# The last FFN's second product by Strassen's seven half products, with the sums on GpSimd

## The chip, the core and the metric

The program runs on one core of one Trainium2 chip. A core has TensorE for matmuls (PE in the profile, its weight loads PEld), VectorE (DVE), ScalarE (ACT), GpSimd (POOL) and SyncE (SP, which here only issues transfers). The engines run beside each other, each takes its own instructions in the order of its queue, and semaphores make one wait for another. Operands lie in SBUF, sums of matmuls in the eight banks of PSUM (128 rows of 512 float32 each), and weights come by DMA from the chip's memory. The metric is the device time of one execution, in microseconds.

## What is computed

A two-layer trunk over 512 tokens of width 1024: a gated short convolution, a dense FFN, a Mamba-2 mixer, a dense FFN. Norms, a scale, a shift and a gate stand around each. Only the second FFN (i = 1) is touched. Everything is float32.

```
D_FF = 2816

def swiglu_ffn(h, w_in, w_out):
    gate, up = jnp.split(h @ w_in, 2, axis=-1)
    return (jax.nn.silu(gate) * up) @ w_out

h = rmsnorm(x, norm_g[i, 2]) * (1.0 + scale) + shift
y = swiglu_ffn(h, f_w_in[i], f_w_out[i])
x = x + gate * rmsnorm(y, norm_g[i, 3])
```

## The kernel before

Every large product is made with float32r operands and keeps float32's accuracy by a split: a value v is cast to hi (float32r) by ScalarE, and VectorE subtracts, lo = v - hi. A product is then three matmuls into the same PSUM bank: hi by hi, hi by lo, lo by hi (lines 259 to 261 in `mm3`, 359 to 361 in `mm_tiles`). `split_w` (lines 202 and 203) splits a piece of 1024 columns of weights.

The last FFN is `ffn(3, 1, ...)`. Its first product goes over 22 blocks of 128 hidden values, two at a time (a pair): `load_w` fetches gate and up columns, `in_chunk` makes 8 x 3 matmuls of 512 tokens for each block of each half, 24 matmuls a chunk and four chunks a pair. `ff_act` applies silu on ScalarE (line 826), multiplies by up on VectorE (827), and splits the hidden value into hi and lo (829, 830). All 22 split blocks stay in SBUF.

The second product, 512 tokens x 2816 by 2816 x 1024, is `out_begin` and `out_finish`. It runs in two halves of 512 output columns. In each half four PSUM banks hold the four token tiles of 128, and the loop goes over the 22 blocks: `load_wo` fetches up to four blocks of 128 x 512 weights (1 MB, issued by SP), splits them two blocks at a time, and each block makes 4 x 3 matmuls: stationary a 128 x 128 piece of the hidden block, moving 512 columns of weights. That is 22 x 4 x 2 x 3 = 528 matmuls. The last two blocks of the first half and the last four of the second are ordered token tile by token tile (`finish`), so that the square sums (`sq`), the gate product (`yg_`), the root (`b1`, `rt1`, `rc1`), the update of x (`x`) and its store of one tile stand beside the matmuls of the next.

The order on TensorE is that of the code where `manual_schedule` names it, elsewhere the tile framework's scheduler sets it; it also sets the order on ScalarE, VectorE, GpSimd and SP around the second product. Buffers come from pools that rotate: `wst` (two), `whl` (four), `h0` to `h7` (the split input of the first product), `t2` (four). GpSimd has nothing to do after the constants at the start.

Of the kernel before, what the change touches and what calls it, by code (L numbers as in the profile page):

```python
# [35 lines left out]
def trunk_kernel(  # L36
# [75 lines left out]
    xt = [hp.tile([P, D], F32, name=f"x{t}", tag=f"x{t}") for t in range(4)]  # L112
# [172 lines left out]
    def small(n):  # L285
        return tmp.tile([P, n], F32, tag=f"ss{n}", name="ss", bufs=8)
# [257 lines left out]
    with ExitStack() as ph:  # L544
# [18 lines left out]
        h = [hp.tile([P, 2, T], F32R, tag=f"h{j}", name=f"h{j}") for j in range(4)]  # L563
        rows = actp.tile([P, 8, P], F32, tag="a", name="rows")
# [254 lines left out]
        def ffn(s, i, begun, act_tile, gg_tile, xn_tile, ada, gates, lead, after):  # L819
            w1, w2 = f_w_in[i], f_w_out[i]  # L820
            acts = []
            h, lead_ps, rest, more = begun

            def ff_act(psg, psu, f):
                g = t2("g")
                act.activation(g, psg, AF.Silu)  # L826
                dve.tensor_mul(g, psu, g)  # L827
                a = act_tile(f"ff{f}")
                act.copy(a[:, 0, :], g)
                dve.tensor_tensor(a[:, 1, :], g, a[:, 0, :].bitcast(F32), SUB)  # L830
# [34 lines left out]
    with ExitStack() as ph:  # L865
# [359 lines left out]
        with tc.manual_schedule(engines={PE_ENGINE}):  # L1225
# [56 lines left out]
```

## Time and profile before

| | us |
|---|---|
| median of 3 runs (lowest, highest) | 1391.58 (1391.44, 1391.78) |
| span of the profiled execution | 1390.8 |
| PE busy in it | 1368.9 (98%) |
| PEld busy | 1148.8 (83%) |
| DVE busy | 832.2 (60%) |
| ACT busy | 552.4 (40%) |
| POOL busy | 1.5 (0%) |

The span runs from the first to the last instruction of one profiled execution; the profile gives no other time of that execution, and the median of the runs is 0.8 us above it. PE's busy time counts matmuls that overlap, so it says whether TensorE has work, not how fast it goes; for that, starts are compared. The mean granted clock over the span is 0.996 of full. A share of the whole span mixes many stages; the stage in question is the last 125 us. In rows of the views, "L203" is a line of the kernel, out<-in are tile names, x is a count, "us, ns" are the sum and the mean of one instruction, and behind the second bar stands how long the engine was idle before them and what ended that.

### The profile page before, as it was taken

To read this page: it belongs to the slowest core of one execution; us is meant where nothing else is said; L and a number is where in the kernel's file an instruction comes from. 1 tells how busy PE (TensorE), PEld (TensorE's weight loads), DVE (VectorE), ACT (ScalarE), POOL (GpSimd) and SP (SyncE) were. 2 spreads that over 40 slices of the span, in tenths; PEclk is the share of its full clock that TensorE was granted. 3 is DMA by queue.
4 is the path that set the end of the run, shared out by engine and by line. 5 is a ranking of instruction groups with operands and counts; after the bars stand their busy time and mean duration, and the time that the engine had idled before them with its cause. 6 is when DMAs were issued, how large, how long until landed. Compare 5 with 4: busy or idle time off the path is not lost.

```text
span 1390.8 us, 17396 instructions
## 1 busy us (share of the span) xinstructions
PE 1368.9 (98%) x7039; PEld 1148.8 (83%) x7039; DVE 832.2 (60%) x1332; ACT 552.4 (40%) x827; POOL 1.5 (0%) x11
## 2 busy tenths in 40 slices
PE   8999999999999999999799999999999999999998
PEld 7788889888888888898688888888898888888886
DVE  5777756488775222759878888876673333332224
ACT  5432247222222211745765466643573222322212
POOL 0000000000000000000000000000000000000000
PEclk9999999999999999999999999999999999999999
DMA  9956671368683223415244432423413223322221
GB/s 313 317 175 223 221 239 42 120 210 287 219 272 122 91 91 98 118 48 179 70 133 136 129 98 83 131 76 107 137 60 106 91 91 101 109 93 91 91 91 61
DMA packets 154037, 190.35 MB, mean 137 GB/s; under 512 B 5845, under 2 KB 110949, under 8 KB 152933
## 3 DMA queue, kind: packets, MB, share of 16 engines
q1 hardware_dynamic: 149952, 176.47, 39.2%
q10 hardware_dynamic: 4004, 12.77, 2.8%
q8 instruction: 55, 0.90, 0.3%
q14 instruction: 26, 0.20, 0.1%
HBM read 186.98 MB, written 2.24 MB: 136 GB/s over the span
## 4 chain that ended last, share of the span: by engine, by line
PE 66%; DVE 1%; issue 0%; DVEq 0%; ACT 0%; ACTq 0%
PE ip L259 11%; PE ip L261 11%; PE ip L260 11%; PE y L359 8%; PE y L360 8%; PE y L361 8%; PE li L259 2%; PE li L261 2%; PE li L260 2%; PE yd L1092 1%; PE yo L1086 1%; PE cb L1036 1%; PE xtr L460 1%; PE ssg L1114 0%; PE xtok L1019 0%; PE st L1051 0%
## 5 line engine op out<-in xcount | busy, mean ns | idle before, releaser
L259 PE MATMUL ip<-h,whl 128*128 128x512 f32 x1096 | 434.2, 396 | 2.7 <-DVE cv L777 2.7
L261 PE MATMUL ip<-h,whl 128*128 128x512 f32 x1096 | 429.4, 392 | 6.6 <-DVE whl L203 6.6
L260 PE MATMUL ip<-h,whl 128*128 128x512 f32 x1096 | 428.2, 391 | 0.0
L261 PEld LDWEIGHTS ip<-h,whl 128*128 128x128 f32 x1096 | 206.6, 188 | 50.7 <-DVE whl L203 7.0
L259 PEld LDWEIGHTS ip<-h,whl 128*128 128x128 f32 x1096 | 206.8, 189 | 47.7 <-issue 5.6
L260 PEld LDWEIGHTS ip<-h,whl 128*128 128x128 f32 x1096 | 206.7, 189 | 43.2 <-issue 1.2
L203 DVE TENSOR_TENSOR whl<-wst,whl 128x1024 fp32r<-128x1024 f32 (+1 forms) x163 | 177.2, 1103 | 101.4 <-ACT whl L202 101.2
L202 ACT CAST whl<-wst 128x1024 fp32r<-128x1024 f32 (+1 forms) x163 | 152.1, 951 | 201.0 <-PE ip L261 121.6
L203 DVE TENSOR_TENSOR whlo<-wsto,whlo 128x1024 fp32r<-128x1024 f32 x68 | 83.3, 1225 | 181.3 <-ACT whlo L202 181.3
L202 ACT CAST whlo<-wsto 128x1024 fp32r<-128x1024 f32 x68 | 71.5, 1051 | 200.6 <-PE y L361 162.2
L359 PE MATMUL y<-whlo,ff 128*128 128x512 f32 x352 | 137.0, 389 | 0.0
L361 PE MATMUL y<-whlo,ff 128*128 128x512 f32 x352 | 136.9, 389 | 0.0
L360 PE MATMUL y<-whlo,ff 128*128 128x512 f32 x352 | 136.9, 389 | 0.0
L126 DVE SCALAR_TENSOR_TENSOR ada_acc<-ada_st,csil,ada_acc 128x512 f32<-128x512 f32 x140 | 104.8, 750 | 22.9 <-DMA ada_st<-in_ada_w_dram 20.0
L259 PE MATMUL li<-h,whl 128*128 128x256 f32 x288 | 83.2, 289 | 0.0
L827 DVE TENSOR_TENSOR g<-ip,g 128x512 f32<-128x512 f32 x40 | 27.6, 691 | 92.5 <-PE ip L261 92.4
L261 PE MATMUL li<-h,whl 128*128 128x256 f32 x288 | 81.6, 283 | 0.0
L260 PE MATMUL li<-h,whl 128*128 128x256 f32 x288 | 81.5, 283 | 0.0
L826 ACT ACTIVATE g<-ip 128x512 f32<-128x512 f32 x36 | 21.6, 599 | 145.9 <-PE ip L261 145.9
L361 PEld LDWEIGHTS y<-whlo,ff 128*128 128x128 f32 x352 | 66.1, 188 | 13.8
L359 PEld LDWEIGHTS y<-whlo,ff 128*128 128x128 f32 x352 | 66.1, 188 | 13.7
L360 PEld LDWEIGHTS y<-whlo,ff 128*128 128x128 f32 x352 | 66.1, 188 | 13.6
(215 smaller groups left out, 1623.2 us busy)
## 6 DMA issues: line engine op xcount, KB each, us to landing
ada_st<-in_ada_w_dram SPq DMA_DIRECT2D x96, 512.0 KB, 5.8
wst<-in_f_w_in_dram SPq DMA_DIRECT2D x44, 1024.0 KB, 5.2
wsto<-in_f_w_out_dram SPq DMA_DIRECT2D x20, 1024.0 KB, 4.9
wst<-in_m_w_in_dram SPq DMA_DIRECT2D x14, 1024.0 KB, 5.4
wst<-in_m_w_in_dram SPq DMA_DIRECT2D x20, 512.0 KB, 5.0
wst<-in_a_w_in_dram SPq DMA_DIRECT2D x9, 1024.0 KB, 6.2
csb<-cs_d ACTq DMA_DIRECT2D x8, 1024.0 KB, 6.2
wsto<-in_m_w_out_dram SPq DMA_DIRECT2D x7, 1024.0 KB, 4.9
```

The costliest lines, as they stand in the source:

```text
L126: dve.scalar_tensor_tensor(acc, w, csil[:, k:k + 1], acc, MUL, ADD)
L202: act.copy(dst[:, 0, :nk, :], src)
L203: dve.tensor_tensor(dst[:, 1, :nk, :], src, dst[:, 0, :nk, :].bitcast(F32), SUB)
L259: pe.matmul(dst, w_at(w, 0, kk), a[:, 0, sl], start=start, stop=False)
L260: pe.matmul(dst, w_at(w, 0, kk), a[:, 1, sl], start=False, stop=False)
L261: pe.matmul(dst, w_at(w, 1, kk), a[:, 0, sl], start=False, stop=stop)
L359: pe.matmul(pst, a[:, 0, tk], wt[:, 0, kk, :], start=k == 0, stop=False)
L360: pe.matmul(pst, a[:, 0, tk], wt[:, 1, kk, :], start=False, stop=False)
L361: pe.matmul(pst, a[:, 1, tk], wt[:, 0, kk, :], start=False, stop=k == K - 1)
L460: pe.transpose(pt[:, j * 256 + t * P:j * 256 + (t + 1) * P], self.xn[2 * hi + t][p // 2][:, c:c + P], ident)
L826: act.activation(g, psg, AF.Silu)
L827: dve.tensor_mul(g, psu, g)
```

## The change

The last FFN gets its own function, `last_ffn`. Its first product is as before, but `ff_pair` leaves the hidden values of a pair unsplit (x0 and x1, 512 tokens each), and GpSimd forms four sums of 256 columns per pair (lines 1266 to 1269 of the changed program). The second product takes the tokens in two halves of 256, the output columns in two halves of 512, and the inner dimension in 11 pairs of blocks: 2 x 2 blocks, which Strassen's algorithm (in Winograd's form) multiplies with seven half products instead of eight. A half product is two token tiles of 128 by 512 columns over 11 blocks: 2 x 3 x 11 = 66 matmuls, so 462 in all.

Six PSUM banks (pa, pb, pz, two each) cannot hold seven products, so the inner dimension is passed three times. The first pass makes three products (pa, pb, pz), and then ScalarE and VectorE copy what the other outputs need (lines 1347 to 1351). The second adds three more onto the same banks; then lines 1381 and 1382 read pb. The third adds the seventh onto pb. In the first and second pass every pair's rows of w2 are loaded (512 KB by line 1293 and 256 KB by 1294, into `raw`, three buffers), and GpSimd forms two sums of 512 columns per pair: line 1330 in place in `raw` and line 1332 from `raw` into `sums` in the first pass; 1362 in place in `raw` and 1366 from `raw` onto `sums` in the second. ScalarE and VectorE split everything for its product only then (`parts`, lines 1298 and 1299): `a6` (hidden values and their sums, in `wst`), `w8` and `w4` (weights and their sums), `a22` for the third pass. At the end the token tiles 0 and 1 are finished beside the third pass, tiles 2 and 3 behind it.

```diff
+        def ff_pair(pss):
+            xs = [pool.tile([P, T], F32, tag=f"xb{b}", name=f"xb{b}", bufs=NG2) for b in range(2)]
+            sm = pool.tile([P, 3, 256], F32, tag="sm", name="sm", bufs=NG2)
+            for b in range(2):
+                g = t2("g")
+                act.activation(g, pss[b], AF.Silu)
+                dve.tensor_mul(xs[b], pss[2 + b], g)
+            pool_tt = nc.gpsimd.tensor_tensor
+            pool_tt(sm[:, 0, :], xs[0][:, hi], xs[1][:, hi], SUB)
+            pool_tt(sm[:, 1, :], sm[:, 0, :], xs[0][:, lo], SUB)
+            pool_tt(sm[:, 2, :], sm[:, 1, :], xs[1][:, lo], ADD)
+            pool_tt(xs[0][:, hi], xs[0][:, lo], xs[0][:, hi], SUB)
...
+        def load_rows(g, b):
+            st = pool.tile([P, 3, T], F32, tag="raw", name="raw", bufs=3)
+            dma(st[:, 0:2, :], w2[rows(g, b), :].rearrange("p (a f) -> p a f", a=2))
+            dma(st[:, 2, :], w2[rows(g, 1 - b), T:])
+            return st
+        def parts(src, dst):
+            act.copy(dst[:, 0], src)
+            dve.tensor_tensor(dst[:, 1], src, dst[:, 0].bitcast(F32), SUB)
...
+        def narrow(early=False):
+            if early:
+                return whl_p.tile([P, 2, T], F32R, tag="whl", name="w4")
+            ring[0] += 1
+            return hp.tile([P, 2, T], F32R, tag=f"h{ring[0] % KD}", name="w4")
...
+        def product(acc, a, i, w, first, last):
+            for t in range(2):
+                sl = slice(t * P, (t + 1) * P)
+                pe.matmul(acc[t], a(0, i, sl), w[:, 0, :], start=first, stop=False, skip_group_check=True)
+                pe.matmul(acc[t], a(0, i, sl), w[:, 1, :], start=False, stop=False, skip_group_check=True)
+                pe.matmul(acc[t], a(1, i, sl), w[:, 0, :], start=False, stop=last, skip_group_check=True)
...
+            for g in range(NG2):
+                st = load_rows(g, 0)
+                a6 = wst_p.tile([P, 2, 3, 256], F32R, tag="wst", name="a6")
+                parts(x0s[g][:, lo], a6[:, :, 0, :])
+                parts(sums[g][:, 0:2, :], a6[:, :, 1:3, :])
+                nc.gpsimd.tensor_tensor(st[:, 1, :], st[:, 1, :], st[:, 0, :], ADD)
+                tw = sums[g][:, 0:2, :].rearrange("p a b -> p (a b)")
+                nc.gpsimd.tensor_tensor(tw, st[:, 1, :], st[:, 2, :], ADD)
+                w8 = whl_p.tile([P, 2, 2, T], F32R, tag="whl", name="w8")
+                parts(st[:, 0, :], w8[:, :, 0, :])
+                w4 = narrow(g < 2)
+                parts(tw, w4)
+                parts(st[:, 1, :], w8[:, :, 1, :])
...
+                product(pa, a, 0, w8[:, :, 0, :], g == 0, True)
+                product(pb, a, 2, w4, g == 0, True)
+                product(pz, a, 1, w8[:, :, 1, :], g == 0, True)
+            np1, nr1, c22 = ([keep(n) for _ in range(2)] for n in ("np1", "nr1", "c22"))
+            for t in range(2):
+                act.activation(np1[t], pa[t], AF.Copy, scale=-1.0)
+            for t in range(2):
+                dve.tensor_tensor(nr1[t], np1[t], pb[t], SUB)
+            for t in range(2):
+                act.copy(c22[t], pz[t])
...
+            for g in range(NG2):
+                st = load_rows(g, 1)
+                a6 = wst_p.tile([P, 2, 3, 256], F32R, tag="wst", name="a6")
+                parts(x1s[g][:, lo], a6[:, :, 0, :])
+                parts(x0s[g][:, hi], a6[:, :, 1, :])
+                parts(sums[g][:, 2, :], a6[:, :, 2, :])
+                w8 = whl_p.tile([P, 2, 2, T], F32R, tag="whl", name="w8")
+                parts(st[:, 0:2, :], w8)
+                nc.gpsimd.tensor_tensor(st[:, 2, :], st[:, 2, :], st[:, 1, :], ADD)
+                w4 = narrow()
+                parts(st[:, 2, :], w4)
+                tw = sums[g][:, 0:2, :].rearrange("p a b -> p (a b)")
+                nc.gpsimd.tensor_tensor(tw, tw, st[:, 0, :], ADD)
+                a22 = pool.tile([P, 2, 256], F32R, tag="xb0", name="a22", bufs=NG2)
+                parts(x1s[g][:, hi], a22)
...
+                todo = [(pa, 0, w8[:, :, 0, :]), (pb, 1, w4), (pz, 2, w8[:, :, 1, :])]
+                if g == NG2 - 1:
+                    todo = [todo[1], todo[0], todo[2]]
+                for acc, i, w in todo:
+                    product(acc, a, i, w, False, True)
...
+            for g in range(NG2):
+                w4 = narrow()
+                parts(sums[g][:, 0:2, :].rearrange("p a b -> p (a b)"), w4)
...
+                product(pb, lambda hl, i, sl, g=g: a22s[g][:, hl, sl], 0, w4, False, True)
...
+            for t in range(4):
+                if t >= 2:
+                    dve.tensor_tensor(np1[t - 2], pb[t - 2], np1[t - 2], SUB)
+                    ys[t] = (np1[t - 2], c22[t - 2])
...
     with ExitStack() as ph:
-        actp3 = ph.enter_context(tc.tile_pool(name="actp3", bufs=22, reuse_waits="tile"))
-        ffn(3, 1, begun, lambda n: actp3.tile([P, 2, T], F32R, tag="a", name=n),
-            lambda: actp3.tile([P, D], F32, tag="gg", name="gg", bufs=1), None, lambda f: None, (), None, None)
+        last_ffn(begun, ph.enter_context(tc.tile_pool(name="lf", bufs=1, reuse_waits="tile")))
```

What the scheduler made of it is seen in the engines' queues. GpSimd, in the first pass, from pair 2 on: the names are `raw` (the loaded rows; 10000, 10036, 10072, 10108 are pairs 2 to 5, and so on in steps of 36) and `sm` (the pair's sums; 8877, 9006, 9135, 9264 are pairs 2 to 5). Before, this queue held nothing behind the constants at the program's start.

```order
L1332 TENSOR_TENSOR sm_8877<-raw_10000 128x512
L1330 TENSOR_TENSOR raw_10108<-raw_10108 128x512
L1332 TENSOR_TENSOR sm_9006<-raw_10036 128x512
L1330 TENSOR_TENSOR raw_10144<-raw_10144 128x512
L1332 TENSOR_TENSOR sm_9135<-raw_10072 128x512
L1332 TENSOR_TENSOR sm_9264<-raw_10108 128x512
L1330 TENSOR_TENSOR raw_10180<-raw_10180 128x512
L1330 TENSOR_TENSOR raw_10216<-raw_10216 128x512
L1332 TENSOR_TENSOR sm_9393<-raw_10144 128x512
L1330 TENSOR_TENSOR raw_10252<-raw_10252 128x512
L1332 TENSOR_TENSOR sm_9522<-raw_10180 128x512
```

The first addition of pair g + 3, whose rows go into the buffer of pair g, stands behind the second addition of pair g and ahead of that of pair g + 1; pairs 4 and 5 have their second additions in a row, pairs 7 and 8 too.

ScalarE, in the second product. Before, the casts of `load_wo`'s pieces follow each other:

```order
L202 CAST whlo_10085<-wsto_10083 128x1024
L202 CAST whlo_10088<-wsto_10083 128x1024
L202 CAST whlo_10141<-wsto_10139 128x1024
L202 CAST whlo_10144<-wsto_10139 128x1024
L202 CAST whlo_10201<-wsto_10199 128x1024
```

Now, in the second pass (raw_10531, 10570 and 10609 are pairs 5, 6 and 7; a6_10495 is pair 4's):

```order
L1298 CAST w8_10541<-raw_10531 128x1024
L1298 CAST a22_10471<-xb1_9005 128x256
L1298 CAST w4_10584<-raw_10570 128x512
L1298 CAST w4_10623<-raw_10609 128x512
L1298 CAST a6_10495<-xb1_9134 128x256
L1298 CAST a6_10495<-xb0_9133 128x256
L1298 CAST a6_10495<-sm_9135 128x256
```

Many small casts have taken the place of a few large ones, and the weights' sum of pair 7 is cast ahead of the hidden values of pair 4.

VectorE, at the program's end. Before, behind the last token tile's matmuls (y03 and y13 are its two halves):

```order
L409 TENSOR_SCALAR ss_10584<-ss_10581 128x1
L404 TENSOR_TENSOR yg_10586<-y03_9914,gg_9781 128x512
L404 TENSOR_TENSOR yg_10602<-y13_10198,gg_9781 128x512
L417 RECIPROCAL ss_10604<-ss_10604 128x1
L421 SCALAR_TENSOR_TENSOR x3_101<-yg_10586,ss_10604,x3_101 128x512
L421 SCALAR_TENSOR_TENSOR x3_101<-yg_10602,ss_10604,x3_101 128x512
```

Now, behind the last product into pb (pb_9924 and pb_9925 are token tiles 2 and 3):

```order
L1398 TENSOR_TENSOR np1_10325<-pb_9925,np1_10325 128x512
L1406 TENSOR_TENSOR yg_10913<-c22_10328,gg_10774 128x512
L1406 TENSOR_TENSOR yg_10912<-np1_10324,gg_10774 128x512
L1410 RECIPROCAL ss_10921<-ss_10921 128x1
L1406 TENSOR_TENSOR yg_10932<-c22_10329,gg_10774 128x512
L1413 SCALAR_TENSOR_TENSOR x2_100<-yg_10913,ss_10921,x2_100 128x512
L1413 SCALAR_TENSOR_TENSOR x2_100<-yg_10912,ss_10921,x2_100 128x512
L1406 TENSOR_TENSOR yg_10931<-np1_10325,gg_10774 128x512
L1408 TENSOR_SCALAR ss_10939<-ss_10930 128x1
L1410 RECIPROCAL ss_10940<-ss_10940 128x1
L1413 SCALAR_TENSOR_TENSOR x3_101<-yg_10932,ss_10940,x3_101 128x512
L1413 SCALAR_TENSOR_TENSOR x3_101<-yg_10931,ss_10940,x3_101 128x512
```

Two token tiles stand behind the last matmul where one half of one stood.

More of the change, by code (lines that the diff above doesn't have):

```diff
@@ L1247, in trunk_kernel, with last_ffn, rows, keep @@
             begun = out_finish(parts)
+    def last_ffn(begun, pool):
+        w1, w2 = f_w_in[1], f_w_out[1]
+        h, lead_ps, rest, more = begun
+        lo, hi = HALVES
+        x0s, x1s, sums = [], [], []
+        def ff_pair(pss):
[10 more added lines that the diff above has]
+            pool_tt(xs[0][:, hi], xs[0][:, lo], xs[0][:, hi], SUB)
+            x0s.append(xs[0])
+            x1s.append(xs[1])
+            sums.append(sm)
+        NG2 = NF // 2
+        for f in range(0, NF, 2):
+            if f == 0:
+                with tc.manual_schedule(engines={PE_ENGINE}):
+                    for i in (0, 2, 1, 3, 4, 5):
+                        rest(i)
+                pss = lead_ps[:4]
+            elif f == 2:
+                pss = lead_ps[4:] + [in_chunk(w, h) for w in more]
+            else:
+                pss = [in_chunk(w, h) for w in load_w([(w1, f * P, 256)]) + load_w([(w1, DFF + f * P, 256)])]
+            ff_pair(pss)
+        def rows(g, b):
+            return slice((2 * g + b) * P, (2 * g + b + 1) * P)
+        def load_rows(g, b):
[6 more added lines that the diff above has]
+            dve.tensor_tensor(dst[:, 1], src, dst[:, 0].bitcast(F32), SUB)
+        ring = [0]
+        def narrow(early=False):
[3 more added lines that the diff above has]
+            return hp.tile([P, 2, T], F32R, tag=f"h{ring[0] % KD}", name="w4")
+        def keep(name):
+            return pool.tile([P, T], F32, tag="keep", name=name, bufs=6)
+        def product(acc, a, i, w, first, last):
[4 more added lines that the diff above has]
+                pe.matmul(acc[t], a(1, i, sl), w[:, 0, :], start=False, stop=last, skip_group_check=True)
+        ggt = []
+        with tc.manual_schedule(engines={PE_ENGINE}):
+            pa = [aux_ps("pa") for _ in range(2)]
+            pb = [aux_ps("pb") for _ in range(2)]
+            pz = [mm_ps("pz") for _ in range(2)]
+            for g in range(NG2):
[11 more added lines that the diff above has]
+                parts(st[:, 1, :], w8[:, :, 1, :])
+                def a(hl, i, sl):
+                    return a6[:, hl, i, sl]
+                product(pa, a, 0, w8[:, :, 0, :], g == 0, True)
[8 more added lines that the diff above has]
+                act.copy(c22[t], pz[t])
+            a22s = []
+            for g in range(NG2):
[13 more added lines that the diff above has]
+                parts(x1s[g][:, hi], a22)
+                a22s.append(a22)
+                def a(hl, i, sl):
+                    return a6[:, hl, i, sl]
+                todo = [(pa, 0, w8[:, :, 0, :]), (pb, 1, w4), (pz, 2, w8[:, :, 1, :])]
[3 more added lines that the diff above has]
+                    product(acc, a, i, w, False, True)
+            for t in range(2):
+                nr2 = t2("nr2")
+                dve.tensor_tensor(nr2, np1[t], pb[t], SUB)
+                dve.tensor_tensor(c22[t], nr2, c22[t], ADD)
+            ops = []
+            for g in range(NG2):
+                w4 = narrow()
+                parts(sums[g][:, 0:2, :].rearrange("p a b -> p (a b)"), w4)
+                ops.append(w4)
+                if g == 0:
+                    ggt.append(make_gg(3, lambda: pool.tile([P, D], F32, tag="raw", name="gg", bufs=3)))
+                product(pb, lambda hl, i, sl, g=g: a22s[g][:, hl, sl], 0, w4, False, True)
+            for t in range(2):
+                dve.tensor_tensor(nr1[t], nr1[t], pz[t], ADD)
+            ys = [(pa[0], nr1[0]), (pa[1], nr1[1]), None, None]
+            for t in range(4):
+                if t >= 2:
+                    dve.tensor_tensor(np1[t - 2], pb[t - 2], np1[t - 2], SUB)
+                    ys[t] = (np1[t - 2], c22[t - 2])
+                s2 = small(2)
+                yg = [t2("yg") for _ in range(2)]
+                order = (1, 0) if t >= 2 else (0, 1)
+                for hf in order:
+                    act.activation(t2("junk"), ys[t][hf], AF.Square, accum_out=s2[:, hf:hf + 1])
+                for hf in order:
+                    dve.tensor_mul(yg[hf], ys[t][hf], ggt[0][:, hf * T:(hf + 1) * T])
+                b1, s1 = small(1), small(1)
+                dve.tensor_scalar(b1, s2[:, order[0]:order[0] + 1], 1.0 / D, EPS, MUL, ADD)
+                act.activation(s1, s2[:, order[1]:order[1] + 1], AF.Sqrt, bias=b1, scale=1.0 / D)
+                dve.reciprocal(s1, s1)
+                for hf in order:
+                    c = slice(hf * T, (hf + 1) * T)
+                    dve.scalar_tensor_tensor(xt[t][:, c], yg[hf], s1, xt[t][:, c], MUL, ADD)
+                    dma(out[0, t * P:(t + 1) * P, c], xt[t][:, c])
```

## The prediction

> **What bounds the kernel now.** First the busy time by stretches, cut where the last FFN's second product begins and ends (columns: stretch, its length, then busy us and instructions of PE, PEld, DVE, ACT, POOL, then the granted clock, the DMA share and GB/s).
>
> ```profile
> 1243.00:1264.00 21.00, 21.00 (x94) 17.38 (x93) 7.16 (x8) 5.94 (x8) 0.00 (x0) 1.00 0.29 100
> 1264.00:1384.00 120.00, 120.00 (x530) 99.10 (x528) 33.94 (x41) 27.42 (x38) 0.00 (x0) 1.00 0.24 82
> 1384.00:1391.00 7.00, 0.07 (x1) 0.00 (x0) 2.17 (x4) 0.98 (x3) 0.00 (x0) 0.89 0.29 110
> ```
>
> TensorE works all 120 us of the second product at full clock, VectorE 34, ScalarE 27, GpSimd nothing. A matmul less is worth its interval there, as long as the others keep up. The groups by line give the count, the timeline the interval.
>
> ```profile
> L359 PE MATMUL y<-whlo,ff 128*128 128x512 f32 x176 | 68.5, 389 | 0.0
> L360 PE MATMUL y<-whlo,ff 128*128 128x512 f32 x176 | 68.5, 389 | 0.0
> L361 PE MATMUL y<-whlo,ff 128*128 128x512 f32 x176 | 68.5, 389 | 0.0
> ```
>
> ```profile
> 1264.23 0.39 PE L359 MATMUL y<-whlo,ff 128*128 128x512 f32 x1
> ...
> 1383.68 0.39 PE L361 MATMUL y<-whlo,ff 128*128 128x512 f32 x1
> ```
>
> 528 matmuls whose starts span 119.45 us: one every 119.45 / 527 = 0.2267 us (the 389 ns of one overlap).
>
> **What goes.** Seven products for eight leave 11 pairs x 7 x 6 = 462 matmuls of the same form: 66 fewer, 66 x 0.2267 = **15.0 us** off TensorE. A pair's three products in the first or second pass take 18 x 0.2267 = 4.08 us, a pass 44.9, the third pass 15.0.
>
> **What comes: the prices.** The splits (a cast by ScalarE, then a subtraction by VectorE) at their three widths, from the groups by line:
>
> ```profile
> L203 DVE TENSOR_TENSOR whlo<-wsto,whlo 128x1024 fp32r<-128x1024 f32 x19 | 23.3, 1226 | 75.7 <-ACT whlo L202 75.7
> L202 ACT CAST whlo<-wsto 128x1024 fp32r<-128x1024 f32 x19 | 20.0, 1054 | 82.2 <-PE y L361 74.5 <-PE ip L261 3.9 <-issue 3.9
> L830 DVE TENSOR_TENSOR ff<-g,ff 128x512 fp32r<-128x512 f32 x22 | 15.0, 685 | 2.5 <-ACT ff L829 2.5
> L829 ACT CAST ff<-g 128x512 fp32r<-128x512 f32 x22 | 13.5, 616 | 0.0
> L478 DVE TENSOR_TENSOR h<-u,h 128x256 fp32r<-128x256 f32 x3 | 1.3, 425 | 0.5 <-ACT h L474 0.5
> L474 ACT CAST h<-u 128x256 fp32r<-128x256 f32 x2 | 0.8, 407 | 1.3 <-DVE u L469 1.3
> ```
>
> A first-pass pair splits 256 + 4 x 512 columns: ScalarE 0.41 + 4 x 0.62 = 2.9 us, VectorE 0.43 + 4 x 0.69 = 3.2. A second-pass pair splits 3 x 256, 1024, 512 and 256: ScalarE 3.3, VectorE 3.6; from pair 4 on a third-pass split of 512 stands among them (3.9 and 4.3). Against 4.08 that is nearly full but hidden, and rows that follow each other overlap a little:
>
> ```profile
> 1264.43 0.69 DVE L827 TENSOR_TENSOR g<-ip,g 128x512 f32<-128x512 f32 x1 [2.48 <-PE ip L261]
> 1265.56 1.23 DVE L203 TENSOR_TENSOR whlo<-wsto,whlo 128x1024 fp32r<-128x1024 f32 x1 [0.44 <-ACT whlo L202]
> 1266.71 0.68 DVE L830 TENSOR_TENSOR ff<-g,ff 128x512 fp32r<-128x512 f32 x1
> ```
>
> The second subtraction starts 1.15 us after one of 1.23. The splits of the hidden values (L829, L830) move here from the first product, where TensorE was the bound anyway; nothing is gained there.
>
> GpSimd gets 44 additions of 256 columns in the first product, a set per 96 matmuls or 21.8 us, hidden, and **44 of 512 columns** in the second. The trace has no such operation. Its nearest rows:
>
> ```profile
> L566 POOL MEMSET rows<- 128x256 f32 x1 | 0.3, 314 | 0.0
> masks.py:66 POOL TENSOR_SCALAR_AFFINE_SELECT mask<-mask 128x128 f32<-128x128 f32 x1 | 0.3, 297 | 0.0
> ...
> L70 POOL MEMSET ones<- 128x128 f32 x1 | 0.2, 206 | 0.0
> ```
>
> Writing alone costs 0.108 us per 128 columns over 0.10 fixed; reading one and writing one costs 0.20. So each stream takes about 0.1 per 128 columns. An addition has three streams: 0.10 + 4 x 0.30 = **1.3 us**, the value I take (call it p). Bounds: 0.53 if it ran like the memset, 1.69 if each input passed like a whole select. Two additions per pair are 2.6 us, under 4.08: the load alone would be hidden. The Trainium skill (GPSIMD Engine Reference, "3.1 Elementwise — side-by-side cycle accounting") gives 4497 ns for this addition at 2048 columns; a quarter of that is an estimate of 1.1 us, by which the sum below would be some 4 us less. No run here shows it.
>
> Weights come as 512 + 256 KB per pair, into three buffers:
>
> ```profile
> wsto<-in_f_w_out_dram SPq DMA_DIRECT2D x10, 1024.0 KB, 4.9
> ...
> wsto<-in_f_w_out_dram SPq DMA_DIRECT2D x2, 512.0 KB, 3.7
> ```
>
> ```profile
> 1266.82 0.37 SPq L229 DMA_DIRECT2D wsto<-in_f_w_out_dram  x1
> ```
>
> The buffer's last reader (L203 above, 1265.56 + 1.23) ended 0.03 us before SP issued. From a freed buffer to the first 512 KB landed I take 3.7 + 0.1 = **3.8 us**. SP has these loads in the order in which the buffers come free, and nothing else until the end. 22 x 0.79 MB in some 130 us are 133 GB/s where the stretch had 82. Other stretches of this kernel reach far more (last column), so I cost no contention:
>
> ```profile
> 65.00:70.00 5.00, 5.00 (x17) 3.92 (x16) 5.00 (x10) 1.75 (x4) 0.00 (x0) 0.66 1.08 360
> ```
>
> **First pass: a ring on GpSimd's queue.** The rows of the change show it. The second addition of a pair (L1332) is the last reader of its buffer, which pair g+3 then loads. But in GpSimd's queue the first addition of pair g+3 (L1330) stands ahead of L1332 of pair g+1, and pb's product of pair g+1 waits for that. So L1332 to L1332 takes 3.8 + 2p = 6.4 us, against 4.08 on TensorE. Where two L1332 stand in a row (pairs 4 and 5, 7 and 8), the second waits for its pair's a6 split, which ScalarE takes after the w4 cast before it: 0.62 + 0.41 + 0.62 + 0.69 + p = 3.6, then 6.4: 10.0 for two pairs. From pair 2 to pair 10 there are four single steps and two double: 4 x 6.4 + 2 x 10.0 = 45.6 us, TensorE's pace would be 8 x 4.08 = 32.6. Ahead of it, pair 2's L1332 ends at 8.7 (a6's buffer is free when pair 0 ends at 4.1, plus 0.2; two w8 casts 1.2, a6 casts 1.0, VectorE's queue to 7.4, p). Behind it come the w4 split (1.4) and 12 matmuls (2.7). The pass ends 58.4 us after its start, not 44.9: **+13.5**. With p at 0.53 it is +3.5 (then TensorE's pace is the longer in the double steps), at 1.69 it is +19.5.
>
> **Second pass.** L1362 and L1366 free the buffer sooner, and the queue keeps pace, with two exceptions on ScalarE: the w4 cast of pair 7 stands ahead of the a6 casts of pair 4, that of pair 10 ahead of pair 7's. Pair 7's buffer is pair 4's, freed by VectorE 2.7 us after pair 2's products begin (cast 1.05, subtraction 1.23, queue); then 3.8 + 2p + cast 0.62 + a6 0.41 + 0.43 = 10.6 us after that beginning, where pair 4 was due at 8.16: 2.4 late; pair 10's is 1.7 late by the same count. At the pass's start the copies of pa and pz (L1347, L1351) stand behind casts that wait for GpSimd: 1. Together **+5** (2 to 8 with p). The third pass waits for nothing: its splits are done by then or 5 us ahead.
>
> **The end.** Before, only one half of one token tile hung on the last matmuls; now the last product feeds two tiles. From the trace:
>
> ```profile
> L421 DVE SCALAR_TENSOR_TENSOR x<-yg,ss,x 128x512 f32<-128x512 f32 x8 | 5.7, 748 | 0.1
> L404 DVE TENSOR_TENSOR yg<-y,gg 128x512 f32<-128x512 f32 x8 | 5.5, 686 | 4.9 <-ACT junk L400 4.9
> ...
> L414 ACT ACTIVATE ss<-ss 128x1 f32<-128x1 f32 x4 | 1.2, 294 | 0.1
> ...
> L417 DVE RECIPROCAL ss<-ss 128x1 f32<-128x1 f32 x4 | 0.6, 156 | 0.9 <-ACT ss L414 0.9
> ...
> L409 DVE TENSOR_SCALAR ss<-ss 128x1 f32<-128x1 f32 x4 | 0.6, 148 | 5.2 <-ACT junk L400 5.2
> ```
>
> ```profile
> 1264.00 0.39 PE L261 MATMUL ip<-h,whl 128*128 128x512 f32 x1
> ...
> 1385.98 1.41 DVE L421 SCALAR_TENSOR_TENSOR x<-yg,ss,x 128x512 f32<-128x512 f32 x2
> ```
>
> VectorE ended 1387.39 - 1383.68 = 3.7 us after the last matmul's start. Now, after the first np1, its queue holds np1, four yg, two reciprocals, one scalar operation, four updates (0.71 each) and a wait for one square root: 0.43 + 0.69 + 2.74 + 0.31 + 0.15 + 2.82 + 0.29 = 7.4 us, the 0.43 being what L827 waited after the start of the matmul at 1264.00. That is 3.7 more, and the first np1 is read 0.1 late: **+3.8**.
>
> **The sum.** -15.0 + 13.5 + 5 + 3.8 = +7.3 us. The profiled span is 1390.8, 0.8 under the median of the three runs (1391.58); the terms are differences, so they go on the median: **1399 us**, 0.5% slower. With p the sum moves about 18 us per us.
>
> **Rival 1: GpSimd and VectorE exclude each other.** Every split reads two SBUF operands, so does every addition. If one had to stand still while the other runs, their times would add: first pass 3.2 + 2.6 = 5.8 per pair, second 3.6 + 2.6 = 6.2, and eight third-pass splits: 63.5 + 68.3 + 5.5 = 137, less 13 done before the pass begins (pairs 0 and 1) = 124, plus the third pass 15: 139 against 119.7, and the end 3.8: +23, **1415 us**. Against it and for it the trace has nothing: GpSimd is idle wherever VectorE works. The Trainium skill (SBUF — State Buffer, "Who interferes with whom") states just this: a VectorE instruction with two SBUF inputs and a GpSimd instruction that reads SBUF lock each other out for the whole instruction. No run here shows it.
>
> **Rival 2: the additions are cheap, and it is faster.** At p = 0.53 the ring is 3.8 + 1.06 = 4.9, the first pass loses 3.5, the second 2: -15.0 + 3.5 + 2 + 3.8 = -5.7, **1386 us**. Place: L1330 and L1332 in the first pass. It decides at p = 0.73 (VectorE's own price is 0.69): below, it is faster by over 0.2%; from there to 1.04, no change. For it: the memset's row. Against: the select, with one input, already comes to 0.10 + 4 x 0.20 = 0.90 for 512 columns.
>
> **Rival 3: the clock.** A wait of 2.74 us was followed by a lower clock here:
>
> ```profile
> 64.66 0.47 PE L259 MATMUL ip<-h,whl 128*128 128x512 f32 x1 [2.74 <-DVE cv L777]
> ```
>
> The clock of the stretch from 65 to 70 us, quoted with the transfers above, was 0.66: over 5 us that is 3.4 us at half rate, 1.7 us lost. My stalls are 2.3 us. In the first pass the ring would hide it (4.08 + 1.7 is under 6.4); two stalls in the second would add 3.4: 1402, inside the forecast's own range.
>
> **How the numbers follow.** Forecast with p above 1.04: 0.46 (1394 to 1407). Rival 1: 0.23. p from 0.73 to 1.04, no change: 0.11. Rival 2: 0.20. The likeliest is 1399; the range runs from 1385 to 1417. Within 0.2% (2.8 us, about what a measurement tells from no change): 0.11; slower 0.46 + 0.23 = 0.69; faster 0.20.
>
> **What would show it.** Right: 462 matmuls 0.227 us apart; in the first pass TensorE idle before pb's products, released by VectorE's w4 split, about 2.3 us at pairs 3, 4, 7 and 10 and 1 or less at the others; GpSimd's L1332 about 6.4 us apart; two stalls before a6 in the second pass; the last VectorE instruction 7.4 us after the last matmul's start. Wrong: additions well under 1 us, loads that land sooner, or VectorE's subtractions longer than 0.69 us while GpSimd works (rival 1).

## The result, and the profile after

| | before | after |
|---|---|---|
| median, us (lowest, highest) | 1391.68 (1391.44, 1392.14) | 1411.67 (1410.16, 1412.37) |
| ratio to before, 95% interval | | 1.0137 (1.0123 to 1.0152) |
| span of the profiled execution, us | 1390.8 | 1408.4 |

The change costs 20.0 us where the forecast was 7.4. The profiled execution of after is the fastest of its four (1410.16), and 1.8 us of its time lie outside the span, so the two spans differ by less, 17.5 us before rounding; the parts below add up to that.

The stretches of after, cut at its three passes (same columns as in the prediction: PE, PEld, DVE, ACT, POOL busy, clock, DMA share, GB/s):

```profile
1263.00:1323.20 60.20, 51.54 (x199) 38.84 (x198) 45.35 (x52) 29.67 (x55) 36.67 (x26) 0.94 0.37 132
1323.20:1383.50 60.30, 50.89 (x200) 38.72 (x199) 48.48 (x77) 33.24 (x71) 27.14 (x17) 0.94 0.28 100
1383.50:1398.50 15.00, 15.00 (x67) 12.20 (x65) 9.12 (x19) 6.07 (x14) 0.00 (x0) 1.00 0.19 71
```

The first matmul of each pass and the last of all, from the timeline of after:

```profile
1263.01 0.39 PE L1315 MATMUL pa<-w,a 128*128 128x512 f32 x1
...
1323.32 0.39 PE L1315 MATMUL pa<-w,a 128*128 128x512 f32 x1
...
1383.51 0.39 PE L1315 MATMUL pb<-w,a 128*128 128x512 f32 x1
...
1398.24 0.39 PE L1317 MATMUL pb<-w,a 128*128 128x512 f32 x1
```

Against 44.9 us unstalled, the first pass takes 60.3 (+15.4), the second 60.2 (+15.3); the third takes 14.7 and loses nothing. The second product starts 1.2 earlier than before, and from the last matmul's start to the end of the span it is 10.1 us instead of 7.1 (+3.0). With the 15.0 that seven products save: -15.0 + 15.4 + 15.3 + 3.0 - 1.2 = 17.5.

What TensorE waited for most in these passes (sum, times, longest), and the groups of VectorE's splits and GpSimd's 512-column additions, of after:

```profile
PE pb L1315 <- ACT w L1298: 6.5, 5, 1.6
PE pa L1315 <- ACT a L1298: 3.5, 3, 2.1
PE pa L1317 <- DVE a L1299: 3.2, 2, 1.7
PE pb L1315 <- DVE nr L1349: 2.7, 2, 2.2
```

```profile
L1299 DVE TENSOR_TENSOR w<-raw,w 128x512 fp32r<-128x512 f32 x29 | 31.2, 1088 | 18.6 <-ACT w L1298 17.8
L1299 DVE TENSOR_TENSOR a<-xb,a 128x256 fp32r<-128x256 f32 x42 | 22.5, 555 | 0.4
...
L1366 POOL TENSOR_TENSOR sm<-sm,raw 128x512 f32<-128x512 f32 x11 | 20.0, 1822 | 19.5 <-DMA raw<-in_f_w_out_dram 19.4
L1362 POOL TENSOR_TENSOR raw<-raw 128x512 f32<-128x512 f32 x11 | 15.9, 1446 | 0.0
L1332 POOL TENSOR_TENSOR sm<-raw 128x512 f32<-128x512 f32 x9 | 15.6, 1729 | 7.0 <-DVE a L1299 7.0
L1330 POOL TENSOR_TENSOR raw<-raw 128x512 f32<-128x512 f32 x7 | 9.5, 1352 | 21.4 <-DMA raw<-in_f_w_out_dram 21.4
```

The waits name the splits, as the prediction had it in the first pass. But the splits themselves are longer than those of before: 1.09 us in the mean for the 29 of 512 columns that read `raw`, where 512 columns took 0.69 before, and 0.56 for 256 that took 0.43; and the same addition of GpSimd takes 1.35 us in one line and 1.82 in another. That is rival 1's mark. The timeline shows it one by one, GpSimd first, then VectorE:

```profile
1334.15 4.02 POOL L1366 TENSOR_TENSOR sm<-sm,raw 128x512 f32<-128x512 f32 x1 [4.97 <-DMA raw<-in_f_w_out_dram]
1338.13 1.28 POOL L1362 TENSOR_TENSOR raw<-raw 128x512 f32<-128x512 f32 x1
```

```profile
1333.26 0.68 DVE L1299 TENSOR_TENSOR w<-raw,w 128x512 fp32r<-128x512 f32 x1
1333.86 0.74 DVE L1299 TENSOR_TENSOR a<-xb,a 128x256 fp32r<-128x256 f32 x2
1334.53 0.41 DVE L1299 TENSOR_TENSOR a<-sm,a 128x256 fp32r<-128x256 f32 x1
1334.87 1.81 DVE L1299 TENSOR_TENSOR w<-raw,w 128x512 fp32r<-128x512 f32 x2
1336.61 0.41 DVE L1299 TENSOR_TENSOR a<-xb,a 128x256 fp32r<-128x256 f32 x1
```

While VectorE works without a gap from 1333.26 to 1337.02, one addition takes 4.02 us, and the next, with VectorE at rest, 1.28. The wait is inside the instruction's duration and counts as busy: no view lists it as idle.

### The profile page after: what moved, and what is told of

It is laid out like the page before. It is cut to its first block, busy times and chain, and to the rows that moved or that the text cites. A ratio compares the mean times of both kernels' runs of the same rounds, so it can differ in the third digit from the quotient of the medians.

```text
span 1408.4 us, 17625 instructions
## 1 busy us (share of the span) xinstructions
PE 1364.2 (97%) x6973; PEld 1137.8 (81%) x6973; DVE 896.7 (64%) x1430; ACT 586.6 (42%) x919; POOL 110.1 (8%) x99
## 4 chain that ended last, share of the span: by engine, by line
PE 59%; DVE 3%; POOL 2%; DMA 2%; issue 1%; ACT 0%; POOLq 0%; DVEq 0%; SPq 0%; ACTq 0%
PE ip L259 11%; PE ip L261 11%; PE ip L260 11%; PE y L359 5%; PE y L361 5%; PE y L360 5%; PE li L259 2%; PE li L261 2%; PE li L260 2%; DMA raw<-in_f_w_out_dram 2%; PE yd L1092 1%; DVE a L1299 1%; POOL sm L1332 1%; PE yo L1086 1%; DVE w L1299 1%
## 5 line engine op out<-in xcount | busy, mean ns | idle before, releaser
L203 DVE TENSOR_TENSOR whl<-wst,whl 128x1024 fp32r<-128x1024 f32 (+1 forms) x163 | 179.5, 1117 | 102.0 <-ACT whl L202 101.7
L203 DVE TENSOR_TENSOR whlo<-wsto,whlo 128x1024 fp32r<-128x1024 f32 x46 | 56.3, 1224 | 96.7 <-ACT whlo L202 96.7
L1266 POOL TENSOR_TENSOR sm<-xb,xb 128x256 f32<-128x256 f32 x11 | 8.6, 782 | 1189.6 <-DVE xb L1264 1189.6
L202 ACT CAST whlo<-wsto 128x1024 fp32r<-128x1024 f32 x46 | 48.3, 1050 | 113.8 <-PE y L361 87.8
L957 DVE SCALAR_TENSOR_TENSOR cu<-ip,cols,cu 128x511 f32<-128x511 f32 (+2 forms) x84 | 62.0, 740 | 14.4 <-ACT cu L954 14.2
L359 PE MATMUL y<-whlo,ff 128*128 128x512 f32 x176 | 68.6, 390 | 0.0
L361 PE MATMUL y<-whlo,ff 128*128 128x512 f32 x176 | 68.5, 389 | 0.0
L360 PE MATMUL y<-whlo,ff 128*128 128x512 f32 x176 | 68.5, 389 | 0.0
L1299 DVE TENSOR_TENSOR w<-raw,w 128x512 fp32r<-128x512 f32 (+1 forms) x44 | 47.7, 1098 | 21.6 <-ACT w L1298 20.8
L259 PEld LDWEIGHTS li<-h,whl 128*128 128x128 f32 x288 | 55.3, 192 | 0.0
L260 PEld LDWEIGHTS li<-h,whl 128*128 128x128 f32 x288 | 55.2, 192 | 0.0
```

What stands on the lines that cost most here:

```text
L202: act.copy(dst[:, 0, :nk, :], src)
L203: dve.tensor_tensor(dst[:, 1, :nk, :], src, dst[:, 0, :nk, :].bitcast(F32), SUB)
L259: pe.matmul(dst, w_at(w, 0, kk), a[:, 0, sl], start=start, stop=False)
L260: pe.matmul(dst, w_at(w, 0, kk), a[:, 1, sl], start=False, stop=False)
L359: pe.matmul(pst, a[:, 0, tk], wt[:, 0, kk, :], start=k == 0, stop=False)
L360: pe.matmul(pst, a[:, 0, tk], wt[:, 1, kk, :], start=False, stop=False)
```

## The experiments

Three theories. **Lock**: a VectorE subtraction of two SBUF operands and a GpSimd addition exclude each other, instruction by instruction. **Ring**: only the prediction's forecast, the order of GpSimd's queue with three raw buffers and the price of an addition. **Clock**: the stretches at half clock that follow stalls add on their own. All results stand in one table; the ratio is to before on the same chip, "second product" is the time from its first to its last matmul's start, and "addition" is the mean of GpSimd's 512-column additions that start in the second product (for "sums made earlier", of all of them, which stand in the first).

| kernel | median, us | ratio to before (95%) | second product, us | addition, us |
|---|---|---|---|---|
| before | 1391.68 | | 119.5 | |
| after | 1411.67 | 1.0137 (1.0123 to 1.0152) | 135.2 | 1.61 |
| no sums | 1379.56 | 0.9907 (0.9890 to 0.9923) | 104.5 | |
| additions nobody waits for | 1399.56 | 1.0052 (1.0037 to 1.0067) | 124.0 | 1.61 |
| split operand in PSUM | 1391.24 | 0.9992 (0.9982 to 1.0002) | 115.8 | 1.30 |
| its twin in SBUF | 1408.16 | 1.0117 (1.0102 to 1.0132) | 132.9 | 1.76 |
| sums by VectorE | 1383.08 | 0.9929 (0.9915 to 0.9942) | 107.2 | |
| sums made earlier | 1384.43 | 0.9936 (0.9923 to 0.9948) | 108.8 | 1.45 |
| additions in pair order | 1413.66 | 1.0148 (1.0132 to 1.0164) | 137.0 | 1.62 |
| pair order and PSUM operand | 1385.31 | 0.9945 (0.9929 to 0.9961) | 109.5 | 1.30 |
| memsets for additions | 1380.93 | 0.9912 (0.9893 to 0.9931) | 104.5 | |

The scheduler sets the order on the other engines anew for each kernel, so a difference of 1 or 2 us between two of them may be order alone. The kernels ran on several chips, on which the median of before lay between 1391.7 and 1393.7; the differences of medians given below are within 1 us of what the ratios say.

**No sums.** What do the additions cost in all?

```diff
-                nc.gpsimd.tensor_tensor(st[:, 1, :], st[:, 1, :], st[:, 0, :], ADD)
-                nc.gpsimd.tensor_tensor(tw, st[:, 1, :], st[:, 2, :], ADD)
...
-                nc.gpsimd.tensor_tensor(st[:, 2, :], st[:, 2, :], st[:, 1, :], ADD)
...
-                nc.gpsimd.tensor_tensor(tw, tw, st[:, 0, :], ADD)
```

> The 44 GpSimd additions of 512 columns in the second product are left out (the weights' sums are not formed; the splits read what stands in the buffers), so nothing of the first two passes waits for GpSimd. All theories give the same here, as it measures the whole price of these additions: 1391.6 - 15.0 (66 matmuls) + 3.8 (end) + 1 (start of the second pass) = 1381 us, 30 us under the change. VectorE's 512-column subtraction should be back at 0.69 us. Above 1386, something else than GpSimd costs (the weights' transfers, ScalarE or VectorE at 4 us of work per 4.08 us pair).

1379.56: 32 us under after, 1.4 under the time expected. TensorE never waits; 462 matmuls take 104.5 us, which is 461 intervals of 0.2267. So the 15.0 of the prediction were exact, and all that the change gives back is due to the additions, the longer end apart.

**Additions nobody waits for.** Is it enough that GpSimd works, though no data hangs on it?

```diff
-                nc.gpsimd.tensor_tensor(st[:, 1, :], st[:, 1, :], st[:, 0, :], ADD)
-                nc.gpsimd.tensor_tensor(tw, st[:, 1, :], st[:, 2, :], ADD)
+                junk = pool.tile([P, T], F32, tag="junk", name="junk", bufs=1).rearrange("p (a b) -> p a b", a=2)
+                for i in range(2):
+                    nc.gpsimd.tensor_tensor(junk, a6[:, i, 0:2, :].bitcast(F32), xh, ADD)
```

(and the same in the second pass; `xh` is 512 columns of x). One tie is left: a6 has two buffers, and one comes free only when GpSimd has read it.

> The same GpSimd load, but nobody waits for it: the 44 additions of 512 columns read a pair's already cast a6 and the residual stream and write a scrap tile (the weights' sums are not formed). Theory lock (a VectorE subtraction of two SBUF operands and a GpSimd addition exclude each other): subtractions of 512 columns stay at 1.0 us or more in the mean, additions above 1.5, a pair costs up to 3.4 + 2.6 = 6 us of the two engines together against 4.08 on TensorE, and the time is 1395 to 1410 though no data depends on GpSimd. Theory ring (only the queue order, three raw buffers and the price of an addition cost): subtractions at 0.69, additions at 1.28, 1381 to 1384 us.

Two groups of this kernel, a split's and an addition's:

```profile
L1299 DVE TENSOR_TENSOR w<-raw,w 128x1024 fp32r<-128x1024 f32 x11 | 23.0, 2093 | 0.1
...
L1366 POOL TENSOR_TENSOR junk<-a,x 128x512 f32<-128x512 f32 x22 | 33.8, 1537 | 24.0 <-DVE a L1299 15.2 <-ACT a L1298 8.7
```

1399.56, 20.0 us more than without the additions, and the 1024-column split takes 2.09 us where it took 1.23 before. The granted clock is 1.00 in both passes. In the first pass (49.6 us) ScalarE waits three times for an addition that still reads the a6 buffer it needs, 7.6 us in all. In the second (59.7 us, 14.8 more than unstalled) no engine waits for an addition and GpSimd is idle for 24 us before them, yet VectorE is busy for 59.5 of the 59.7 us. So the lock by itself costs the 14.8 us of the second pass, nearly what after loses there (15.3); how much of the first pass's 4.7 is the a6 buffer was not tried.

**Split operand in PSUM, and its twin.** If the lock comes from VectorE's second read of SBUF, one operand in PSUM should end it with everything else in place.

```diff
+                other = fill[0][:, :n]
...
+                dve.tensor_tensor(dst[:, 1], other, dst[:, 0].bitcast(F32), SUB)
...
+                if g == 0:
+                    dz = mm_ps("dz")
+                    pe.matmul(dz, a(0, 0, slice(0, P)), w8[:, 0, 0, :], start=True, stop=True)
+                if g == 1:
+                    fill.append(dz)
```

The twin appends `xt[0][:, :T]` (SBUF) in place of `dz`.

> From pair 2 of the first pass on, VectorE's split subtractions take a bank of PSUM in place of the weights or hidden values as their first operand (the low halves are wrong values, all else runs as in the change), so each reads SBUF once. GpSimd's work, its data and its queue are those of the change. Lock: additions fall to 1.3 us (1.45 to 1.82 in the change), subtractions of 512 columns to about 0.7 (1.09 in the change), the second pass loses about 5 us where it lost 15, time 1397 to 1402. Ring alone: additions and time as in its twin with the SBUF operand, about 1411.

> Twin of the kernel with the PSUM operand: the same subtractions take 512 columns of the residual stream in SBUF as first operand (the low halves are wrong values), so each reads SBUF twice as in the change and waits for the same things as the twin. Lock and ring alike: 1408 to 1414 us, additions 1.45 to 1.8 us, as in the change; the difference to the twin is what the place of one operand costs.

The additions of the PSUM kernel, then two of the twin's:

```profile
L1379 POOL TENSOR_TENSOR sm<-sm,raw 128x512 f32<-128x512 f32 x11 | 14.3, 1302 | 13.1 <-DMA raw<-in_f_w_out_dram 13.1
L1375 POOL TENSOR_TENSOR raw<-raw 128x512 f32<-128x512 f32 x11 | 14.3, 1298 | 0.0
L1340 POOL TENSOR_TENSOR sm<-raw 128x512 f32<-128x512 f32 x9 | 11.6, 1292 | 3.8 <-ACT a L1298 3.8
L1338 POOL TENSOR_TENSOR raw<-raw 128x512 f32<-128x512 f32 x7 | 9.1, 1297 | 21.9 <-DMA raw<-in_f_w_out_dram 21.9
```

```profile
L1379 POOL TENSOR_TENSOR sm<-sm,raw 128x512 f32<-128x512 f32 x11 | 24.8, 2254 | 14.4 <-DMA raw<-in_f_w_out_dram 14.4
L1375 POOL TENSOR_TENSOR raw<-raw 128x512 f32<-128x512 f32 x11 | 17.6, 1600 | 0.0
```

Where one operand lies is worth 1408.16 - 1391.24 = 16.9 us. With PSUM all four lines of additions take 1.29 to 1.30 us in the mean; with SBUF up to 2.25. The lock is shown, with its condition: VectorE reading SBUF twice. (The twin's second product has two stretches of 3.4 us at half clock, the PSUM kernel's none, so up to 3.4 of the 16.9 us may be the clock's.) The PSUM kernel came out 6 us faster than the 1397 to 1402 expected, because that sum took the ring at the prediction's size. What the ring costs alone is seen here: the passes begin at 1265.93, 1318.39 and 1367.03, so the first takes 52.5 (0.2 of it the extra matmul) and the second 48.6, losses of 7.3 and 3.7.

**Additions in pair order, with the lock and without.** The ring cut: GpSimd's queue is pinned to the order of the code.

```diff
-        with tc.manual_schedule(engines={PE_ENGINE}):
+        with tc.manual_schedule(engines={PE_ENGINE, mybir.EngineType.Pool}):
```

> GpSimd takes its additions in the order of the pairs (L1330 and L1332 of pair g, then of pair g+1; L1362, then L1366), so that no L1332 stands behind an addition whose weights it must first free: the ring of the first pass is cut, the lock stays. Ring as the whole cause of the first pass's loss: the second product loses only the 5 us of the second pass, 1386 to 1390. Lock: a first-pass pair still needs 3.2 us of VectorE and 2.6 us of GpSimd one after the other, and the additions stay at 1.45 us or more: 1398 to 1408.

> Ring cut and lock taken away together: GpSimd in the order of the pairs, and VectorE's split subtractions from pair 2 on with an operand in PSUM (the low halves are wrong values). If ring and lock are all that the additions cost, this comes near the kernel without sums though GpSimd makes all 44 additions at 1.3 us: 1380 to 1384 us. If it stays at 1390, the first pass's remaining loss isn't the order of GpSimd's queue.

With the lock, cutting the ring gains nothing (1413.66, 6 above the range expected); without it, it gains 6 us (1391.24 to 1385.31, 1.3 above the range expected; here the PSUM operand is added to the edit). The first pass, from its first matmul's start to that of the next pass, in us, where 44.9 is TensorE's pace:

| | GpSimd's queue as scheduled | in pair order |
|---|---|---|
| two operands in SBUF | 60.3 (after) | 59.7 |
| one operand in PSUM | 52.5 | 46.5 |

Either cause alone stretches the pass, and they do not add: the lock without the ring costs nearly as much as both. Both passes of the locked kernel in pair order, then the first 45.1 us of the one without lock:

```profile
1264.80:1324.30 59.50, 48.64 (x199) 36.27 (x197) 44.44 (x52) 29.27 (x54) 36.70 (x26) 1.00 0.39 132
1324.30:1387.00 62.70, 53.94 (x198) 41.28 (x199) 52.68 (x77) 34.37 (x73) 29.11 (x18) 0.86 0.29 99
```

```profile
1264.40:1309.50 45.10, 45.10 (x200) 37.09 (x198) 28.40 (x47) 27.91 (x51) 29.55 (x25) 1.00 0.48 164
```

Free of the lock, VectorE is busy 29.5 us and GpSimd 30.9 in the whole first pass of 46.5; with it 44.6 and 36.9 in 59.7. The extra 21 us of "busy" are, but for one VectorE instruction more, waits for each other. The locked kernel's second pass ran at a clock of 0.86, which is 62.7 x 0.14 = 8.8 us of lost clock; in after the two passes lost 60.2 x 0.06 + 60.3 x 0.06 = 7.2. The clock thus explains at most 1.6 us between the two kernels, and without it cutting the ring under the lock would have left the time about where it was. One round of the locked first pass, GpSimd, then VectorE:

```profile
1293.26 1.28 POOL L1332 TENSOR_TENSOR sm<-raw 128x512 f32<-128x512 f32 x1 [2.45 <-issue]
1294.51 1.73 POOL L1330 TENSOR_TENSOR raw<-raw 128x512 f32<-128x512 f32 x1
1298.68 1.73 POOL L1332 TENSOR_TENSOR sm<-raw 128x512 f32<-128x512 f32 x1 [2.45 <-issue]
```

```profile
1293.41 1.68 DVE L1299 TENSOR_TENSOR w<-raw,w 128x512 fp32r<-128x512 f32 x1 [0.28 <-ACT w L1298]
1295.24 1.55 DVE L1299 TENSOR_TENSOR w<-sm,w 128x512 fp32r<-128x512 f32 x1
1296.92 0.69 DVE L1299 TENSOR_TENSOR w<-raw,w 128x512 fp32r<-128x512 f32 x1
```

The subtraction at 1293.41 meets an addition that ends at 1294.54 and takes 1.68 instead of 0.69; the addition at 1294.51 then meets that subtraction and takes 1.73 instead of 1.28; the subtraction at 1295.24 ends 0.55 after that addition. Each stands still for the rest of the other's instruction. From L1332 to L1332 it is 5.4 us, against TensorE's 4.08.

**Memsets for additions.** Does any GpSimd instruction lock, or only one that reads?

```diff
-                nc.gpsimd.tensor_tensor(st[:, 1, :], st[:, 1, :], st[:, 0, :], ADD)
-                nc.gpsimd.tensor_tensor(tw, st[:, 1, :], st[:, 2, :], ADD)
+                for _ in range(8):
+                    nc.gpsimd.memset(x0s[g][:, lo], 0.0)
```

(and `x1s[g][:, lo]` in the second pass.)

> In place of the two additions a pair GpSimd fills dead halves of the hidden values, eight times 256 columns (8 x 0.31 = 2.5 us a pair against 2.6 for two additions), once the pair's a6 is split; it reads nothing, and nobody waits for it (the weights' sums are not formed). Lock on reading, as the Trainium skill has it (SBUF — State Buffer, "Who interferes with whom": a VectorE instruction with two SBUF inputs is held up by a GpSimd instruction that reads SBUF, not by one that only writes): 1380 to 1382 us, subtractions of 512 columns at 0.69. Lock on any GpSimd instruction: 1395 to 1402, as with additions that nobody waits for.

```profile
L1363 POOL MEMSET xb<- 128x256 f32 x88 | 27.5, 313 | 17.4 <-DVE a L1299 12.9
L1331 POOL MEMSET xb<- 128x256 f32 x72 | 22.5, 312 | 12.7 <-DVE a L1299 9.1
...
L1299 DVE TENSOR_TENSOR w<-raw,w 128x512 fp32r<-128x512 f32 x29 | 20.1, 721 | 3.4 <-ACT w L1298 3.3
```

1380.93, TensorE never waits: of some 52 us of memsets 43 lie beside a split and cost nothing, and the split's 0.72 us is that of the kernel without sums. Of the two GpSimd instructions tried, only the one that reads takes part in the lock.

**Sums by VectorE.** Two engines that exclude each other are no help to one another; so let the cheaper one do it all. The edit is `dve` for `nc.gpsimd` in the four additions.

> The 44 additions of 512 columns go from GpSimd to VectorE, nothing else changes. Lock: two engines that exclude each other are no faster than one of them, and VectorE's price for such an operation is 0.69 us against 1.3, so the second product gets faster than in the change although VectorE is now the only one to work: 4.6 us a pair in the first pass, 5.0 in the second, plus third-pass splits of 0.7 from pair 4 on, against 4.08 on TensorE; 11 x 4.6 + 11 x 5.0 less 9 done ahead is 97 against 89.8, 6 to 11 us over the 1379.6 without sums: 1386 to 1391. Ring without lock: GpSimd's help is lost and VectorE is the bound, 1405 or more.

```profile
1263.90:1309.00 45.10, 44.55 (x194) 35.93 (x193) 42.86 (x72) 29.45 (x56) 3.69 (x4) 1.00 0.46 157
1309.00:1356.00 47.00, 46.12 (x204) 37.70 (x203) 47.00 (x90) 34.12 (x71) 0.00 (x0) 1.00 0.44 147
```

```profile
1325.05 0.69 DVE L1366 TENSOR_TENSOR sm<-sm,raw 128x512 f32<-128x512 f32 x1
1325.65 0.43 DVE L1299 TENSOR_TENSOR a<-xb,a 128x256 fp32r<-128x256 f32 x1
1325.99 1.23 DVE L1299 TENSOR_TENSOR w<-raw,w 128x1024 fp32r<-128x1024 f32 x1
1327.12 0.69 DVE L1362 TENSOR_TENSOR raw<-raw 128x512 f32<-128x512 f32 x1
```

1383.08: 28.6 us under after and 0.7% faster than before, the fastest kernel here that computes what before computes. VectorE is full in the second pass (47.0 of 47.0 us). It is 3 us better than the range expected. The sum behind that range took whole durations, which may be why: instructions in a row start 0.60, 0.34 and 1.13 us apart where they last 0.69, 0.43 and 1.23, so each costs about 0.09 less.

**Sums made earlier.** GpSimd keeps its work, but in the first product, where VectorE has room; the sums wait in a scratch buffer in memory.

```diff
+        def pre(g):
...
+            tt(b[:, 1, :], a[:, 1, :], a[:, 2, :], ADD)
+            tt(a[:, 1, :], a[:, 1, :], a[:, 0, :], ADD)
+            tt(a[:, 2, :], a[:, 1, :], a[:, 2, :], ADD)
+            tt(b[:, 0, :], a[:, 2, :], b[:, 0, :], ADD)
+            dma(sd[g, :, 0:2, :], a[:, 1:3, :])
+            dma(sd[g, :, 2:4, :], b[:, 0:2, :])
```

> GpSimd keeps the 44 additions of 512 columns, but makes them during the first product, where VectorE is busy a third of the time; the sums go to a scratch buffer in memory and the second product loads them as it loads weights (256 to 512 KB in place of weights, and 256 KB more per pair in the second pass). All else as in the change. Lock: the two engines meet seldom and only where TensorE has slack, second product as in the kernel without sums: 1380 to 1383. If the first product slows down (22 MB more of transfers, or VectorE held up there), it shows as a later start of the second product than 1263. Ring without lock gives the same time here; what tells them apart is whether subtractions in the first product are stretched beside additions (0.69 to over 1 us) at no cost in time.

The first product of this kernel, and the split of its weights there:

```profile
1030.00:1263.00 233.00, 233.00 (x1137) 197.57 (x1136) 81.88 (x84) 62.81 (x85) 101.31 (x84) 1.00 0.57 192
```

```profile
L203 DVE TENSOR_TENSOR whl<-wst,whl 128x1024 fp32r<-128x1024 f32 x38 | 54.8, 1450 | 87.0 <-ACT whl L202 87.0
```

The splits are stretched from 1.23 (L203 before) to 1.45 us and TensorE loses nothing, since it doesn't wait for them there. The second product takes 108.8, 4.3 us more than without sums; TensorE's listed waits make up 1.1 of that, and its weight loads list 5.8 us of waits, all for ScalarE and VectorE; why those are late was not tried. At 1384.43 it is 27 us under after and 1.4 above the range expected.

## Why the prediction fell short

- **The saving**, 15.0: right, as the kernels without additions in the way show (104.5 us for 462 matmuls).
- **The price of an addition**, 1.3: right, 1.29 to 1.30 undisturbed, so rival 2 (additions at 0.53) is out. The estimate of 1.1 from the Trainium skill (GPSIMD Engine Reference, "3.1 Elementwise — side-by-side cycle accounting") was 0.2 short.
- **First pass**, +13.5 for the ring, measured +15.4: near in number, and its rows look as forecast (in after L1332 to L1332 takes 6.30 and 6.28 us in the first two single steps, 10.4 and 10.5 in the double ones). But that is luck: the ring alone does not make these steps. Alone, it costs 7.3: its single step is 5.95 us instead of 6.4, as the weights land 3.4 us after the release instead of 3.8, the second L1332 of a double step follows after 2.85 us instead of 3.6, and pair 2's L1332 ends 6.8 us after the pass's start instead of 8.7:

```profile
1271.44 1.29 POOL L1340 TENSOR_TENSOR sm<-raw 128x512 f32<-128x512 f32 x1 [0.69 <-ACT a L1298]
1276.14 1.29 POOL L1338 TENSOR_TENSOR raw<-raw 128x512 f32<-128x512 f32 x1 [3.40 <-DMA raw<-in_f_w_out_dram]
1277.39 1.29 POOL L1340 TENSOR_TENSOR sm<-raw 128x512 f32<-128x512 f32 x1
```

(split operand in PSUM: 1271.44 to 1277.39.) And with the lock in place, cutting the ring does not make the kernel faster.
- **Second pass**, +5, measured +15.3: the step that failed. The sum set VectorE's splits (3.6 to 4.3 us a pair) and GpSimd's additions (2.6) against TensorE's 4.08 each by itself, as if the two ran beside each other and stayed hidden, and charged only the w4 casts ahead of a6 and the start. Without the lock the whole pass loses 3.7, so these two causes are worth no more; the rest is there only with the lock, subtractions and additions waiting for each other, and some of it, up to 3.4 us, may be the clock's. The same step is wrong in the first pass, where the number hides it.
- **The end**, +3.8: the mechanism was right, and it measured 3.0. VectorE's last update runs until 1403.83 + 1.42 = 1405.25, 7.0 us after the last matmul's start, where 7.4 were counted:

```profile
1403.83 1.42 DVE L1413 SCALAR_TENSOR_TENSOR x<-yg,ss,x 128x512 f32<-128x512 f32 x2
```

- **Rival 1**, chance 0.23, 1415 us: this is what happened. Its second product was to take 139 us and took 135.2. The Trainium skill's rule that the prediction quoted for it (SBUF — State Buffer, "Who interferes with whom") agrees with the runs in each clause tried: two SBUF inputs against a reading GpSimd lock (1.76 us an addition), one SBUF input doesn't (1.30), a GpSimd instruction that only writes doesn't. The prediction gave it half the chance of its own sum, though by its own words the trace of before, where GpSimd is idle, spoke neither for nor against it. Without the lock the change would have come out about level with before (0.9992 for the PSUM kernel), not 0.5% slower.
- **Rival 3**, the clock: seen, and no longer small. In after the clock falls to half four times for some 3.4 us, for example

```profile
1302.80:1305.80 3.00, 3.00 (x9) 2.35 (x8) 1.38 (x2) 1.14 (x2) 2.46 (x2) 0.50 0.55 197
1343.70:1346.70 3.00, 3.00 (x8) 2.34 (x7) 3.00 (x4) 2.44 (x7) 1.46 (x2) 0.50 0.00 0
```

At half rate that is 1.7 us each, as priced, and some 7 us in all; they lie within the losses of 15.4 and 15.3. The kernels that hardly stall have none, but the one with additions nobody waits for has none either, and loses 14.8 us in its second pass alone. How much of the change's 20 us is the clock's was not isolated: no run took the slow clock away and left the same stalls.

## What to carry to other kernels

Before work is moved to GpSimd because it idles, look at what VectorE does at that moment: beside subtractions of two SBUF operands a reading GpSimd instruction is no second engine, and the same work on VectorE alone was 28.6 us faster here. Compare the mean duration of one form between two stages or kernels: a wait for the other engine lies inside the duration and appears in no list of idle times. When a term fits in number, test its mechanism too: the ring explained the first pass to 2 us, and cutting it made nothing faster.

## What the runs showed of the hardware

- The two engines do not always take turns. The addition at 1334.15 stood behind VectorE's run of subtractions to its end (4.02 us, 2.7 of them waiting; the longest of the SBUF twin took 6.09); elsewhere, as in the rows of the pinned order, each waited for one instruction of the other's.
- The slow clock came without a wait of 2.7 us, such as the 2.74 us that preceded it in before: the four stretches of after follow waits of 1.4 to 2.1 us, while its longest wait of all, 2.2 us for nr (L1349), is followed by full clock, and so are waits of up to 1.5 us in the kernel with additions nobody waits for. What decides it these runs don't show.
